# Merged-stage weights of a hybrid decoder layer: every second unit is split into high and low parts by two transfers from DRAM instead of by a load, ScalarE and VectorE

## The chip, the core and the metric

The kernel runs on one core of a Trainium2 chip. The metric is the time of one execution on the device in microseconds (us), the median of its runs. Engines are named as in the profile: PE (TensorE matmuls), PEld (its weight loads), DVE (VectorE), ACT (ScalarE), POOL (GpSimd) and SP (SyncE); POOL, SP and ACT also issue DMA transfers, each from a queue of its own.

## The reference

One layer on 256 tokens of width 2048, all in float32. The input projection feeds multi-head latent attention (16 heads) and a short gated convolution. Each branch has an output projection, both are merged by sigmoid gates, and one projection and a norm follow:

```python
h = _rmsnorm(x, pre_norm_g)
proj = jnp.einsum('bsd,de->bse', h, w_in)
(q_a, c_kv, k_rope, z_mla, c_in, b_gate, c_gate, z_conv, g_mla, g_conv) = jnp.split(proj, cuts, axis=-1)
...
y_mla = jnp.einsum('bse,ed->bsd', attn, w_o_mla)
...
y_conv = jnp.einsum('bse,ed->bsd', b_gate * conv * jax.nn.silu(z_conv), w_o_conv)
merged = jax.nn.sigmoid(g_mla) * y_mla + jax.nn.sigmoid(g_conv) * y_conv
out = jnp.einsum('bsd,de->bse', merged, w_out)
x = x + _rmsnorm(out, post_norm_g)
```

The four 2048 x 2048 weights of `g_mla`, `g_conv`, `y_mla` and `y_conv` are those of the merged stage.

## The kernel before

**Products by parts.** TensorE takes float32r operands, which hold fewer bits than float32. So each operand is split into a high part (the value rounded to float32r) and a low part (value minus high part), and a product is three matmuls: high by high, high by low, low by high (`product`). The low part of a weight tile is `wlo`, the high part `whi`.

**Units.** All weights are cut into 193 units of 128 partitions x 2048 columns (1 MB), numbered in the order of use (`plan`, some are smaller). `load_raw` issues the load of a unit into a `raw` tile (three buffers) from SP's queue. `split_unit` makes two halves of 1024 columns: for each, ACT writes `whi` by a copy that rounds (`split_act`, line 245 in the profile), and DVE writes `wlo` by a subtraction (line 246). `whi` and `wlo` have five buffers each, one per half, used in turn. `take(i)` asks for the raw loads up to unit i+2 and the splits up to unit i+1, then hands the pieces to the matmuls; all matmuls are issued at line 88.

**Stages.** Units 0 to 12 serve the latent projections, 13 to 112 the heads and the convolution, 113 to 176 the merged stage, 177 to 192 the output projection. The merged stage goes over four columns c of 512 outputs; a column has 16 units, four for each of n = 0 (g_mla), 1 (g_conv), 2 (w_o_mla) and 3 (w_o_conv). `tokens(c, n, cols)` takes the four units kk of one n. A unit holds four blocks of 128 x 512; for t = 0 and t = 1 (128 tokens each) the four blocks are gone through, three matmuls each: 24 matmuls a unit, that read half 0, half 1, half 0, half 1. At the end of a column DVE merges the two token blocks into `sg` tiles and turns them (line 320), and POOL writes each to DRAM in four transfers (`far<-sg`, line 328) and reads it back (`sg<-far`, line 332), all within `turned`.

**Order.** A scheduler sets the order on each engine and adds the semaphore waits; every instruction made under `keep_in_program_order` keeps its place on its engine, as all matmuls and all of POOL's transfers here do. Each engine then goes through its list in that order: an instruction that waits holds those behind it. A tile is given out again when all that read it have finished.

Of the kernel before, what the change touches and what calls it, by code (L numbers as in the profile page):

```python
# [11 lines left out]
F32 = mybir.dt.float32  # L12
F32R = mybir.dt.float32r
I32 = mybir.dt.int32
AF = mybir.ActivationFunctionType
ALU = mybir.AluOpType
PSUM = bass.MemoryType.PSUM

P = 128
# [18 lines left out]
UNIT = 2048  # L38
LINE = 32
HALF = UNIT // 2  # L40
# [42 lines left out]
def tile_layer(ctx: ExitStack, tc: tile.TileContext, xw, w0, xb, x, pos, pvec, post_g, wc, wz, wcv, wkr, wqk, wqr, wv, cwr, wsq, out):  # L83
    nc = tc.nc
# [13 lines left out]
    wpool = ctx.enter_context(tc.tile_pool(name="wpool", bufs=1))  # L98
# [5 lines left out]
    plan = []  # L104

    def add(ap, width=UNIT):
        plan.append((ap, width))
        return len(plan) - 1
# [30 lines left out]
    u_d = [[[add(wsq[n, c, k]) for k in range(4)] for n in range(4)] for c in range(4)]  # L139
# [3 lines left out]
    u_out = {ck: add(wsq[4, ck[0], ck[1]]) for ck in out_order}  # L143

    raws, splits, early = {}, {}, {}
    done = {"raw": 0, "split": 0}

    def load_raw(i):
        ap, w = plan[i]
        t = early.get(i)  # L150
        if t is None:
            t = wpool.tile([P, UNIT], F32, name=f"raw{i}", tag="raw", bufs=3)
        if i == 0:
            pieces = [(S, XW, w0), (XW, 2 * XW, xb[0])]
        elif i in (1, 2):

            pieces = [(j * XW, (j + 1) * XW, xb[2 * i - 1 + j]) for j in range(2)]
        else:
            pieces = [(0, w, ap)]
        for a, b, piece in pieces:  # L160
            nc.sync.dma_start(out=t[:, a:b], in_=piece)
        raws[i] = t
        if i == u_qa[5]:
            tc.keep_in_program_order(nc.sync.dma_start(out=tables_pi, in_=pos))
        if i == u_ckv[1]:
            tc.keep_in_program_order(nc.sync.dma_start(out=x_tok, in_=x))

    def split_unit(i):
        t, w = raws.pop(i), plan[i][1]
        parts = []  # L170
        if i == u_kr:
            t = t[:, :w].rearrange("p (k c) -> p k c", k=KD)
            for h in range(2):
                both = wpool.tile([P, HALF], F32R, name=f"whi{i}_{h}", tag="whi", bufs=5)
                both = both[:, :].rearrange("p (k j c) -> p k j c", k=KD // 2, j=2)
                ks = slice(h * KD // 2, (h + 1) * KD // 2)
                split_act(both[:, :, 0], both[:, :, 1], t[:, ks])
                parts.append(both.rearrange("p k j c -> p k (j c)"))
            splits[i] = parts
            return  # L180
        if i <= u_qa[-1]:

            hi, lo = (wpool.tile([P, HALF], F32R, name=f"{o}{i}", tag=o, bufs=5) for o in ("whi", "wlo"))
            for j in range(2):
                k, o = 2 * i + j, j * XW
                src = x_first if k == 0 else t[:, o : o + S]
                split_scaled(x_both, src, k)
                split_act(hi[:, j * R : (j + 1) * R], lo[:, j * R : (j + 1) * R], t[:, o + S : o + XW], True)
            splits[i] = [(hi, lo)]
            return  # L190
        for h in range(0, w, HALF):
            n = min(HALF, w - h)
            if u_out[3, 0] <= i < u_out[3, 3]:
                hi, lo = (op.tile([P, HALF], F32R, name=f"w{o}{i}_{h}") for o in ("hi", "lo"))
            else:
                hi = wpool.tile([P, HALF], F32R, name=f"whi{i}_{h}", tag="whi", bufs=5)
                lo = wpool.tile([P, HALF], F32R, name=f"wlo{i}_{h}", tag="wlo", bufs=5)
            split_act(hi[:, :n], lo[:, :n], t[:, h : h + n], i == u_head[0][1], i in (u_grp["r", 0], u_grp["v", 0], u_head[0][0]))
            parts.append((hi, lo))
        splits[i] = parts  # L200

    def ahead(i, raw=3, split=1):
        while done["raw"] < min(i + raw, len(plan)):
            load_raw(done["raw"])
            done["raw"] += 1
        while done["split"] < min(i + 1 + split, len(plan)):
            while done["raw"] <= done["split"]:
                load_raw(done["raw"])
                done["raw"] += 1
            split_unit(done["split"])  # L210
            done["split"] += 1
# [32 lines left out]
    def split_act(hi, lo, src, keep=False, later=False):  # L244
        a = nc.scalar.activation(hi, src, AF.Copy)  # L245
        b = nc.vector.tensor_tensor(lo, src, hi.bitcast(F32), op=ALU.subtract)  # L246
        if keep:

            tc.keep_in_program_order(a)
        if keep or later:  # L250
            tc.keep_in_program_order(b)
# [91 lines left out]
    def split_scaled(dst, src, k):  # L343
        if k < 3:

            a = nc.vector.tensor_scalar(dst[:, k, :S], src, col("pre_g", k), None, op0=ALU.mult)
        else:
            a = nc.scalar.activation(dst[:, k, :S], src, AF.Copy, scale=col("pre_g", k))
        tc.keep_in_program_order(a)
        tc.keep_in_program_order(  # L350
            nc.vector.scalar_tensor_tensor(
                dst[:, k, S:], src, col("pre_g", k), dst[:, k, :S].bitcast(F32), op0=ALU.mult, op1=ALU.subtract
            )
        )
# [839 lines left out]
```

## Time and profile before

| | |
|---|---|
| median of 2 runs | 1034.59 us (1034.59 to 1034.6) |
| profiled execution, first to last instruction | 1032.9 us |
| busy in it: PE, PEld | 1026.4 us, 854.6 us |
| busy in it: DVE, ACT, POOL | 687.9 us, 531.3 us, 174.2 us |
| mean granted TensorE clock | 0.999 |
| read from HBM, written | 215.66 MB, 12.58 MB |
| packets of SP's queue, of POOL's queue | 54.4%, 8.9% of the 16 DMA engines' time |

The median lies 1.7 us above the span of the profiled execution: that much of a run lies outside its first and last instruction. Busy time is the union of an engine's instructions, and a matmul's end is modelled, so that PE's share says that work never stopped rather than how fast it went. In lists of groups, `out<-in` names tiles without buffer numbers; the numbers behind the bar are busy time in us, mean ns of one instruction, then the idle time ahead of them and what ended it. In lists of transfers the last number is the median time from issue to landing in us.

### The profile page before, as it was taken

To read this page: it belongs to the slowest core of one execution; us is meant where nothing else is said; L and a number is where in the kernel's file an instruction comes from. 1 tells how busy PE (TensorE), PEld (TensorE's weight loads), DVE (VectorE), ACT (ScalarE), POOL (GpSimd) and SP (SyncE) were. 2 spreads that over 40 slices of the span, in tenths; PEclk is the share of its full clock that TensorE was granted. 3 is DMA by queue.
4 is the path that set the end of the run, shared out by engine and by line. 5 is a ranking of instruction groups with operands and counts; after the bars stand their busy time and mean duration, and the time that the engine had idled before them with its cause. 6 is when DMAs were issued, how large, how long until landed. Compare 5 with 4: busy or idle time off the path is not lost.

```text
span 1032.9 us, 12670 instructions
## 1 busy us (share of the span) xinstructions
PE 1026.4 (99%) x4648; PEld 854.6 (83%) x4648; DVE 687.9 (67%) x973; ACT 531.3 (51%) x750; POOL 174.2 (17%) x324
## 2 busy tenths in 40 slices
PE   9999999999999999999999999999999999999997
PEld 8888888888888888888888888888888888888886
DVE  7588777787687777777777785564455455455562
ACT  7675555655456464564555465344434444443551
POOL 4620421104210223112133120020010001002000
PEclk9999999999999999999999999999999999999999
DMA  9775766558675676857676765565565556558642
GB/s 356 280 257 214 269 215 227 207 191 297 212 252 193 209 279 210 278 184 242 229 271 222 267 217 200 204 222 188 201 218 208 188 202 243 183 187 335 231 165 81
DMA packets 44669, 233.24 MB, mean 226 GB/s; under 512 B 7968, under 2 KB 10656, under 8 KB 21696
## 3 DMA queue, kind: packets, MB, share of 16 engines
q1 hardware_dynamic: 32544, 199.67, 54.4%
q0 software_dynamic: 11632, 29.48, 8.9%
q10 hardware_dynamic: 432, 3.29, 0.8%
q8 instruction: 36, 0.59, 0.2%
q14 instruction: 25, 0.20, 0.1%
HBM read 215.66 MB, written 12.58 MB: 221 GB/s over the span
## 4 chain that ended last, share of the span: by engine, by line
PE 99%; DVE 0%; ACT 0%; issue 0%
PE cv L88 34%; PE sq L88 34%; PE z L88 8%; PE out L88 8%; PE qa L88 2%; PE kn L88 2%; PE qn L88 2%; PE vv L88 2%; PE ckv L88 2%; PE qr L88 1%; PE o L88 1%; PE sw L88 1%; PE sc L88 1%; PE idle L88 0%; PE kr L88 0%; DVE og L1048 0%
## 5 line engine op out<-in xcount | busy, mean ns | idle before, releaser
L246 DVE TENSOR_TENSOR wlo<-raw,whi 128x1024 fp32r<-128x1024 f32 (+1 forms) x370 | 440.5, 1196 | 276.6 <-ACT whi L245 265.5
L245 ACT ACTIVATE whi<-raw 128x1024 fp32r<-128x1024 f32 (+1 forms) x372 | 382.7, 1035 | 412.2 <-PE sq L88 180.5
L88 PE MATMUL cv<-whi,x_both 128*128 128x512 f32 x1024 | 319.8, 389 | 0.0
L88 PEld LDWEIGHTS cv<-whi,x_both 128*128 128x128 f32 x1024 | 192.3, 188 | 39.6
L88 PE MATMUL cv<-wlo,x_both 128*128 128x512 f32 x512 | 199.4, 390 | 0.0
L88 PE MATMUL sq<-whi,x_both 128*128 128x512 f32 x512 | 158.2, 389 | 0.0
L88 PEld LDWEIGHTS sq<-whi,x_both 128*128 128x128 f32 x512 | 96.1, 188 | 19.8
L88 PEld LDWEIGHTS cv<-wlo,x_both 128*128 128x128 f32 x512 | 96.1, 188 | 19.3
L88 PE MATMUL sq<-wlo,x_both 128*128 128x512 f32 x256 | 99.6, 389 | 0.0
L88 PE MATMUL z<-whi,x_both 128*128 128x512 f32 x256 | 80.0, 389 | 0.0
L88 PE MATMUL sq<-whi,at_both 128*128 128x512 f32 x256 | 79.4, 389 | 0.0
L88 PE MATMUL sq<-whi,cv_both 128*128 128x512 f32 x256 | 79.4, 389 | 0.0
L88 PE MATMUL out<-whi,m_both 128*128 128x512 f32 x256 | 79.0, 389 | 0.0
L328 POOL DMA_DIRECT2D far<-sg x32 | 17.5, 553 | 305.8 <-DVE sg L320 232.6
L328 POOL DMA_DIRECT2D far<-via x64 | 35.2, 557 | 191.4 <-DVE via L320 190.0
L88 PEld LDWEIGHTS sq<-wlo,x_both 128*128 128x128 f32 x256 | 48.1, 188 | 10.0
L88 PEld LDWEIGHTS out<-whi,m_both 128*128 128x128 f32 x256 | 48.1, 188 | 10.0
L88 PEld LDWEIGHTS sq<-whi,cv_both 128*128 128x128 f32 x256 | 48.1, 188 | 9.9
L88 PEld LDWEIGHTS sq<-whi,at_both 128*128 128x128 f32 x256 | 48.1, 188 | 9.9
L88 PEld LDWEIGHTS z<-whi,x_both 128*128 128x128 f32 x256 | 48.1, 188 | 9.9
L88 PE MATMUL z<-wlo,x_both 128*128 128x512 f32 x128 | 49.8, 389 | 0.0
L88 PE MATMUL sq<-wlo,at_both 128*128 128x512 f32 x128 | 49.8, 389 | 0.0
(227 smaller groups left out, 1131.3 us busy)
## 6 DMA issues: line engine op xcount, KB each, us to landing
raw<-wsq_dram SPq DMA_DIRECT2D x80, 1024.0 KB, 4.8
raw<-wcv_dram SPq DMA_DIRECT2D x64, 1024.0 KB, 5.5
raw<-wz_dram SPq DMA_DIRECT2D x16, 1024.0 KB, 4.8
raw<-wqk_dram SPq DMA_DIRECT2D x8, 1024.0 KB, 6.1
cw<-cwr_dram POOLq DMA_DIRECT2D x24, 256.0 KB, 5.8
raw<-wc_dram SPq DMA_DIRECT2D x4, 1024.0 KB, 9.8
raw<-wv_dram SPq DMA_DIRECT2D x4, 1024.0 KB, 5.3
far<-via POOLq DMA_DIRECT2D x64, 48.0 KB, 4.1
```

The costliest lines, as they stand in the source:

```text
L88: return tc.keep_in_program_order(nc.tensor.matmul(*a, **kw))
L245: a = nc.scalar.activation(hi, src, AF.Copy)
L246: b = nc.vector.tensor_tensor(lo, src, hi.bitcast(F32), op=ALU.subtract)
L328: tc.keep_in_program_order(queue.dma_start(out=f[i], in_=m))
```

## The change

In the merged stage every unit with an odd number (32 of the 64: kk = 0 and 2 of each n) gets no raw load and no split by ACT and DVE. For each of its halves POOL issues a transfer from the weights in DRAM into the `whi` tile, whose type float32r is to round; ACT writes minus `whi` into `wlo`; then POOL issues a second transfer of the same weights that adds them to what stands in `wlo`. The even units are loaded and split as before, and the matmuls are the same.

```diff
     def load_raw(i):
         ap, w = plan[i]
+        if by_transfers(i):
+            return
         t = early.get(i)
...
+    def by_transfers(i):
+
+        return u_d[0][0][0] <= i < u_out[0, 0] and i % 2 == 1
+
+    def split_by_transfers(i):
+
+        ap, parts = plan[i][0], []
+        for h in range(0, UNIT, HALF):
+            hi = wpool.tile([P, HALF], F32R, name=f"whi{i}_{h}", tag="whi", bufs=5)
+            lo = wpool.tile([P, HALF], F32R, name=f"wlo{i}_{h}", tag="wlo", bufs=5)
+            src = ap[:, h : h + HALF]
+            tc.keep_in_program_order(nc.gpsimd.dma_start(out=hi[:, :], in_=src))
+            nc.scalar.activation(lo[:, :], hi[:, :].bitcast(F32), AF.Copy, scale=-1.0)
+            tc.keep_in_program_order(nc.gpsimd.dma_start(out=lo[:, :], in_=src, accum_op=ALU.add))
+            parts.append((hi, lo))
+        splits[i] = parts
+
     def split_unit(i):
+        if by_transfers(i):
+            split_by_transfers(i)
+            return
         t, w = raws.pop(i), plan[i][1]
```

The lines behind these move down by 22, so that ACT's copy of an even unit is line 267 after the change, DVE's subtraction 268, and POOL's turns 350 and 354; the new transfers are lines 181 and 183, the negation 182. In the names below `whi135_1024` is the high part of half 1 (columns 1024 on) of unit 135, and `far_6185` a tile in DRAM. DMASW are the semaphores of POOL's transfers, DMAHW those of SP's.

POOL's list at the end of column 0, from the second token block's turn on; before:

```order
L328 DMA far_6185<-sg1_1_5885 32x4x128 [waits DVE_49]
L328 DMA far_6185<-sg1_1_5885 32x4x128
L328 DMA far_6185<-sg1_1_5885 32x4x128 [waits DMASW1_49]
L328 DMA far_6185<-sg1_1_5885 32x4x128 [waits DMASW2_49]
L332 DMA sg0_0_5733<-far_6181 128x512 [waits DMASW5_49,DMASW6_49,DMASW4_49,DMASW3_49]
L332 DMA sg0_1_5735<-far_6185 128x512 [waits DMASW2_49,DMASW7_49,DMASW1_49,DMASW0_49]
L328 DMA far_6765<-sg1_0_6480 32x4x128 [waits DVE_49]
```

The same place after the change:

```order
L350 DMA far_6185<-sg1_1_5885 32x4x128 [waits DMASW6_49]
L354 DMA sg0_0_5733<-far_6181 128x512 [waits DMASW2_49,DMASW7_49,DMASW1_49,DMASW0_49]
L354 DMA sg0_1_5735<-far_6185 128x512 [waits DMASW5_49,DMASW6_49,DMASW4_49,DMASW3_49]
L181 DMA whi131_0_6232<-wsq_dram 128x1024 [waits PE_49]
L183 DMA wlo131_0_6233<-wsq_dram 128x1024 [waits Activation_49]
L181 DMA whi131_1024_6237<-wsq_dram 128x1024 [waits PE_49]
L183 DMA wlo131_1024_6238<-wsq_dram 128x1024 [waits Activation_49]
L181 DMA whi133_0_6300<-wsq_dram 128x1024 [waits PE_49]
```

Before, nothing followed a column's turn until the next column's. Now the transfers of units 131 to 145 stand between them, in pairs, the second of each behind a wait for ACT, and those of unit 131 behind the turn's waits.

ACT's list in column 1, units 135 to 137 (their place in the column is kk = 2, 3 and 0); before:

```order
L245 ACTIVATE whi135_0_6380<-raw135_6344 128x1024 [waits DMAHW7_49]
L245 ACTIVATE whi135_1024_6384<-raw135_6344 128x1024 [waits PE_49]
L245 ACTIVATE whi136_0_6414<-raw136_6378 128x1024 [waits DMAHW0_49,PE_49]
L245 ACTIVATE whi136_1024_6418<-raw136_6378 128x1024 [waits DVE_49,PE_49]
L245 ACTIVATE whi137_0_6448<-raw137_6412 128x1024 [waits DMAHW1_49,DVE_49,PE_49]
```

The same place after the change:

```order
L182 ACTIVATE wlo135_0_6379<-whi135_0_6378 128x1024 [waits DMASW1_49]
L267 ACTIVATE whi136_0_6412<-raw136_6376 128x1024 [waits DMAHW4_49,PE_49]
L182 ACTIVATE wlo135_1024_6384<-whi135_1024_6383 128x1024 [waits DMASW6_49,DMASW3_49]
L267 ACTIVATE whi136_1024_6416<-raw136_6376 128x1024 [waits PE_49]
L182 ACTIVATE wlo137_0_6447<-whi137_0_6446 128x1024 [waits DMASW5_49,DVE_49,PE_49]
```

The roundings of the even unit stand between the negations of the odd ones, and each negation waits for the landing of its first transfer.

POOL's list at the start of the stage; before:

```order
L777 DMA cw_5445<-cwr_dram 128x512 [waits DMASW6_49,DVE_49]
L328 DMA far_5551<-cw_5549 32x4x128 [waits DVE_49]
L328 DMA far_5551<-cw_5549 32x4x128 [waits DMASW2_49]
L328 DMA far_5551<-cw_5549 32x4x128 [waits DMASW3_49]
L328 DMA far_5551<-cw_5549 32x4x128 [waits DMASW4_49]
```

The same place after the change:

```order
L799 DMA cw_5445<-cwr_dram 128x512 [waits DMASW6_49,DVE_49]
L181 DMA whi113_0_5494<-wsq_dram 128x1024 [waits PE_49,Activation_49]
L183 DMA wlo113_0_5495<-wsq_dram 128x1024 [waits DMASW2_49,Activation_49]
L181 DMA whi113_1024_5499<-wsq_dram 128x1024 [waits DMASW3_49,PE_49]
L181 DMA whi115_0_5619<-wsq_dram 128x1024 [waits DMASW4_49,PE_49]
L183 DMA wlo113_1024_5500<-wsq_dram 128x1024 [waits DMASW5_49,Activation_49]
L183 DMA wlo115_0_5620<-wsq_dram 128x1024 [waits Activation_49]
L350 DMA far_5551<-cw_5549 32x4x128 [waits DMASW7_49,DVE_49]
```

The first transfers of units 113 and 115 stand behind the load of `cw`, and the turn of the last convolution block stands behind them.

## Prediction

> **What bounds the kernel now.** I read the page first: span, busy time, granted clock, and the chain that ended last.
>
> ```profile
> span 1032.9 us, 12670 instructions
> PE 1026.4 (99%) x4648; PEld 854.6 (83%) x4648; DVE 687.9 (67%) x973; ACT 531.3 (51%) x750; POOL 174.2 (17%) x324
> ...
> PEclk9999999999999999999999999999999999999999
> ...
> PE 99%; DVE 0%; ACT 0%; issue 0%
> ```
>
> TensorE works without a gap at its full clock, and the whole chain is TensorE. Nothing that relieves another engine can shorten it; the change can only leave the time alone or open gaps. So the question is whether the weights still arrive in time in the merged stage. Its stretch in the windows view, and the first matmul of column 0 and of column 1 in the timeline of PE:
>
> ```profile
> core 0: us, PE busy (x) PEld busy (x) DVE busy (x) ACT busy (x) POOL busy (x), PEclk, DMA share, GB/s
> 590.00:938.20 348.20, 348.20 (x1537) 288.38 (x1536) 192.78 (x190) 156.25 (x169) 22.29 (x41) 1.00 0.58 206
> ```
>
> ```profile
> 589.79 0.39 PE L88 MATMUL sq<-whi,x_both 128*128 128x512 f32 x1
> ...
> 676.87 0.39 PE L88 MATMUL sq<-whi,x_both 128*128 128x512 f32 x1
> ```
>
> Sixteen units take 676.87 − 589.79 = 87.08 us, so one unit is U = 5.44 us. A unit is read in quarters, half 0, half 1, half 0, half 1 (t = 0, then t = 1). Half 0's buffers come free at 3/4 of the unit, half 1's at its end. The waits of the stage and ACT's timeline show that the splits do wait for these releases, not for weights:
>
> ```profile
> ACT whi L245 <- PE sq L88: 180.2, 109, 3.0
> DVE wlo L246 <- ACT whi L245: 146.7, 70, 2.9
> ```
>
> ```profile
> 675.71 1.06 ACT L245 ACTIVATE whi<-raw 128x1024 fp32r<-128x1024 f32 x1 [3.02 <-PE sq L88]
> 677.07 1.06 ACT L245 ACTIVATE whi<-raw 128x1024 fp32r<-128x1024 f32 x1 [0.30 <-PE sq L88]
> 681.15 1.06 ACT L245 ACTIVATE whi<-raw 128x1024 fp32r<-128x1024 f32 x1 [3.02 <-PE sq L88]
> ```
>
> 677.07 − 675.71 = 1.36 us is a quarter unit, 681.15 − 675.71 = 5.44 a unit. With five buffers, half 0 of unit i takes the buffer of half 1 of unit i−3, free two units (10.88 us) ahead of need. Half 1 takes that of half 0 of unit i−2: free at 3/4 of i−2, needed at 1/4 of i, a lead of one and a half units, 8.16 us. Today a split is 1.06 + 1.22 us of that lead, because the raw weights already lie in SBUF.
>
> **The change, part by part.** It removes 64 subtractions on DVE and 32 loads on SP; from the groups of the stage:
>
> ```profile
> L245 ACT ACTIVATE whi<-raw 128x1024 fp32r<-128x1024 f32 x129 | 136.7, 1059 | 181.0 <-PE sq L88 177.6 <-PE out L88 3.3
> ...
> L246 DVE TENSOR_TENSOR wlo<-raw,whi 128x1024 fp32r<-128x1024 f32 x130 | 159.1, 1224 | 153.0 <-ACT whi L245 147.8
> ```
>
> 64 × 1.224 = 78 us of DVE, all beside TensorE: worth 0. ACT trades 64 roundings for 64 negations of the same shape, priced alike at 1.06 us: 0 by itself. POOL gains 128 transfers, some 0.57 us each to issue (73 us, beside a POOL that is busy for 22 of 348 us). What costs is the order. A half is now made by a chain that starts only when its buffer is free: first transfer (l1, issue to landing), negation, second transfer (l2). I add 0.1 us for each of the two handovers, an estimate, so the negation counts 1.26 us. The five buffers, enough for 2.3 us of splitting, now have to cover two DMA latencies.
>
> l1 and l2 have no row: no 512 KB transfer stands on POOL's queue, and none rounds or adds. The nearest ones, from the list of issues (KB each, median us to landing), then two single ones from narrow windows:
>
> ```profile
> q1 hardware_dynamic: 32544, 199.67, 54.4%
> ...
> raw<-wsq_dram SPq DMA_DIRECT2D x80, 1024.0 KB, 4.8
> ...
> sg<-far POOLq DMA_DIRECT2D x8, 256.0 KB, 5.3
> ...
> at_f<-far_qa SPq DMA_DIRECT2D x1, 512.0 KB, 5.3
> ```
>
> ```profile
> sg<-far POOLq DMA_DIRECT2D x1, 256.0 KB, 3.1
> ```
>
> ```profile
> sg<-far POOLq DMA_DIRECT2D x1, 256.0 KB, 6.9
> ```
>
> SP's queue moves 199.67 MB in 0.544 × 1032.9 us, 355 GB/s, so another 256 KB is 0.74 us. By the sg rows a plain 512 KB transfer then takes 3.8 to 7.6 us, 6.0 at the median. I take l1 = 5.3: the sg rows were measured with a raw load in flight for 4.8 of every 5.44 us, and with half the raw loads I give the 0.74 us back. The second transfer must also read what it adds to: another 512 KB, 1.5 us at the same rate, so l2 = 6.8. Ends: 3.8 for both (reading the target costs nothing) and 7.6 and 9.1; above that no row sets an end if rounding or adding is slow in itself. A gain is excluded, since TensorE has no gap to lose.
>
> Steady state. From the release of half 0 of unit i−2 to half 1 of unit i being ready: l1 + 1.26 + l2; TensorE meets it at 1/4 of unit i, and gives the next buffer of this loop free at 3/4, U/2 = 2.72 us later. So two units take at least 3.98 + l1 + l2 = 16.1 us instead of 10.88: a gap of 5.2 us in every second unit. POOL's queue alone (first transfer, wait for the negation, second issue, twice) needs 2 × (5.3 + 1.26 + 0.57) = 14.3 us, less than that. The DMA engines have, at 355 GB/s, 2.95 us of raw load, 5.9 of the four transfers and 2.95 of targets read in that time, 11.8 us: less as well, though over today's 10.88. 32 × 5.2 = 166 us.
>
> The rounding of the even units stands behind negations that wait for a landing, but its halves have a lead of 8.16 us and more, and need 2.3: cost 0 while the period is stretched anyway.
>
> Column ends. POOL issues unit 129, then both turns of sg, then unit 131 (145 and 147, 161 and 163 alike). The turns in POOL's timeline:
>
> ```profile
> 677.11 2.20 POOL L328 DMA_DIRECT2D far<-sg  x4 [70.77 <-ACT whi L245]
> 681.40 2.17 POOL L328 DMA_DIRECT2D far<-sg  x4 [2.09 <-DVE sg L320]
> 684.21 0.57 POOL L332 DMA_DIRECT2D sg<-far  x1 [0.64 <-DMA far<-sg]
> 688.38 0.57 POOL L332 DMA_DIRECT2D sg<-far  x1 [3.60 <-DMA far<-sg]
> ```
>
> POOL waits for DVE and for landings (the last for 3.60 us) and is free at 688.95, 12.1 us after the column's end at 676.87. Only then starts unit 131: its half 1 is ready 12.1 + 2 × 5.3 + 6.8 + 3.1 (two negations of 1.26 and one issue of 0.57) = 32.6 us after the column's end. With steady gaps alone TensorE would be there after 2.25 U + 2 × 5.2 = 22.6: 10.0 us more, three times, 30 us. The turn after the last column has no transfer behind it.
>
> Start of the stage. Unit 113 stands behind a load of cw on POOL:
>
> ```profile
> 583.22 0.55 POOL L777 DMA_DIRECT2D cw<-cwr_dram  x1 [8.77 <-DVE mv L793]
> ```
>
> From 583.8, half 1 is ready at 583.8 + 10.6 + 6.8 + 3.1 = 604.3, needed at 591.2: 13.1 us, 7.9 over the steady gap.
>
> Sum: 166 + 30 + 8 = 204 us. The profiled span of 1032.9 becomes 1237; the median of the timed runs lies 1.7 above that span, so 1239, said as **1240**.
>
> **The rivals.**
> *Fast transfers.* Every transfer lands like the fastest sg row, 3.8 us for 512 KB. Then two units take 3.98 + 7.7 = 11.7, a gap of 0.8: 25 us; column ends 12.1 + 11.5 + 3.1 − 12.2 − 1.6 = 12.9 each, 39; start 6: about 1105. For it: half the raw loads are gone. Against it: each second transfer shares the engines with the first transfer that POOL issues 0.57 us behind it, and the median of the eight sg rows, at half the bytes, is 5.3.
> The Trainium skill's page "DMA: Bandwidth & Descriptors", section "Anatomy of one DMA — SWDGE (gpsimd) path", gives about 2.0 us plus bytes/436e3 for a transfer from GpSimd: an estimate of 3.2 us for 512 KB, which would leave no steady gap and only the column ends and the start, about 1078 in all. For 256 KB it gives 2.6, and the trace's rows are 3.1 to 6.9; the trace does not bear it out here, and this goes into the same rival.
>
> *Slow rounding or adding.* The nearest rows are plain copies. At 7.6 and 9.1 us two units take 20.7: gaps 9.8, 314 us, column ends 8 each, start 10: 1382. If rounding and adding cost a further 1.5 us each (9.1 and 10.6), two units take 23.7 and the same sum gives about 1475. The profile holds no transfer that rounds or adds, so nothing in it speaks against this; for it speaks only that these are the one kind of work here that no row prices.
>
> *Not slower.* If POOL hands a transfer over with its wait and goes on, no transfer stands behind another's wait, column ends and start cost nothing, and only the loop of half 1 is left. It decides when l1 + 1.26 + l2 is under 8.16 us, so l1 + l2 under 6.9: then 1035. Against it: POOL's 3.60 us idle ahead of sg<-far is such a wait, held on the engine, and even the fastest row doubled is 7.7.
>
> That the first transfer copies bits and rounds nothing would leave wlo at zero and every transfer and wait in place: the same time.
>
> **How the numbers follow.** My case (1150 to 1330 by itself) has 0.55; fast transfers 0.15; slow rounding or adding 0.27; not slower 0.03. The range 1080 to 1430 leaves out the not-slower case and the upper half of the slow one, 0.17 together. A measurement of this kernel can tell about 2% from no change; that is 21 us, and only the last rival stays under it: slower 0.97, same 0.02, faster 0.01.
>
> **What would show it.** The profile after should have PE waits on second transfers (DMA wlo<-wsq_dram) totalling near 200 us, nearly all between 590 and the stage's end, in 32 places at half 1 of odd units; two units 16 us apart; first transfers landing in 5.3 us, second ones in 6.8; three longer gaps of some 15 us behind the sg turns; a TensorE clock as before, DVE 78 us less busy, ACT unchanged. A wrong l1 or l2 moves the time by 32 us per microsecond and more. The prediction is wrong in kind if TensorE waits for even units (ACT's order), or if POOL's queue sets the period of two units.

## The result, and the profile after

| | before | after |
|---|---|---|
| median of 2 runs | 1034.59 us | 1329.14 us (1327.26 to 1331.02) |
| ratio to before, 95% interval | | 1.2848 [1.2804, 1.2891] |
| profiled execution, first to last instruction | 1032.9 us | 1325.5 us |
| merged stage, by its matmuls | 348.2 us | 641.6 us |
| PE busy in it, PE idle in it | 348.2 us, 0 | 424.7 us, 216.9 us |

The page of the kernel after: span, busy time, the slices of PE and of its granted clock, then the chain that ended last.

```profile
span 1325.5 us, 12740 instructions
...
PE 1101.9 (83%) x4648; PEld 896.5 (68%) x4648; DVE 611.0 (46%) x909; ACT 528.7 (40%) x750; POOL 264.9 (20%) x452
...
PE   9999999999999999985676668666475665776998
...
PEclk9999999999999999997888887888787887888999
...
PE 57%; issue 22%; DMA 12%; POOL 4%; ACT 2%; DVE 1%; POOLq 0%; ACTq 0%
```

The first 17 slices are as before; in those of the merged stage, PE works four to eight tenths of the time, and its clock is no longer full. In the chain, DMA, POOL, ACT and issues stand where PE alone stood. The merged stage in the windows view of the kernel after (columns as before):

```profile
core 0: us, PE busy (x) PEld busy (x) DVE busy (x) ACT busy (x) POOL busy (x), PEclk, DMA share, GB/s
589.20:1230.80 641.60, 424.69 (x1539) 331.33 (x1539) 121.53 (x131) 159.90 (x174) 112.57 (x168) 0.82 0.63 165
```

The stage is 641.6 − 348.2 = 293.4 us longer, the whole difference of the spans (292.6). Of this 641.6 − 424.7 = 216.9 us is idle PE, and 424.7 − 348.2 = 76.5 us is the same matmuls taking longer: the granted clock fell from 1.00 to 0.82. What was waited for in the stage, by the waits view (us in total, times, longest):

```profile
POOL wlo L183 <- ACT wlo L182: 434.9, 58, 10.0
...
ACT wlo L182 <- DMA whi<-wsq_dram: 341.0, 53, 16.9
...
PE sq L88 <- DMA wlo<-wsq_dram: 214.1, 38, 8.6
ACT whi L267 <- PE sq L88: 118.1, 44, 11.7
...
POOL whi L181 <- PE sq L88: 16.7, 16, 1.8
```

This is to be read from the bottom of the chain up. PE waits 214 us for second transfers, 38 times. POOL stands 435 us with the second transfer in hand, waiting for the negation; ACT stands 341 us for the first transfer to land. The last row is the telling one: POOL waits only 16.7 us for a buffer. The new transfers in the list of issues:

```profile
raw<-wsq_dram SPq DMA_DIRECT2D x48, 1024.0 KB, 7.0
whi<-wsq_dram POOLq DMA_DIRECT2D x64, 512.0 KB, 6.4
wlo<-wsq_dram POOLq DMA_DIRECT2D x64, 512.0 KB, 5.5
```

One cycle of two units in POOL's timeline (start, duration, idle time ahead and what ended it), and PE and ACT in it:

```profile
1027.02 0.56 POOL L181 DMA_DIRECT2D whi<-wsq_dram  x1 [1.03 <-PE sq L88]
1034.53 0.87 POOL L183 DMA_DIRECT2D wlo<-wsq_dram  x1 [6.96 <-DVE wlo L268]
1035.09 0.85 POOL L181 DMA_DIRECT2D whi<-wsq_dram  x1
1045.43 0.86 POOL L183 DMA_DIRECT2D wlo<-wsq_dram  x1 [9.48 <-ACT wlo L182]
1047.36 0.56 POOL L181 DMA_DIRECT2D whi<-wsq_dram  x1 [1.08 <-PE sq L88]
```

```profile
1042.71 0.80 PE L88 MATMUL sq<-wlo,cv_both 128*128 128x512 f32 x1 [7.59 <-DMA wlo<-wsq_dram]
```

```profile
1032.22 1.06 ACT L267 ACTIVATE whi<-raw 128x1024 fp32r<-128x1024 f32 x1 [2.97 <-PE sq L88]
1033.19 1.04 ACT L182 ACTIVATE wlo<-whi 128x1024 fp32r<-128x1024 f32 x1
1044.07 1.06 ACT L182 ACTIVATE wlo<-whi 128x1024 fp32r<-128x1024 f32 x1 [9.84 <-DMA whi<-wsq_dram]
```

Apart from the 1.08 us at its end, in which POOL waits for a buffer, it issues one transfer or holds the other back all through this cycle of 20.3 us. The cycle is one of column 2; in the other columns two units take about 18.4 us. (The second row names DVE; ACT's negation ended at 1034.23, 0.30 us before the issue.) PE stands for 7.59 us of it.

### The profile page after: what moved, and what is told of

Read it like the earlier page. It is cut to its first block, busy times and chain, and to the rows that moved or that the text cites. A ratio compares the mean times of both kernels' runs of the same rounds, so it can differ in the third digit from the quotient of the medians.

```text
span 1325.5 us, 12740 instructions
## 1 busy us (share of the span) xinstructions
PE 1101.9 (83%) x4648; PEld 896.5 (68%) x4648; DVE 611.0 (46%) x909; ACT 528.7 (40%) x750; POOL 264.9 (20%) x452
## 4 chain that ended last, share of the span: by engine, by line
PE 57%; issue 22%; DMA 12%; POOL 4%; ACT 2%; DVE 1%; POOLq 0%; ACTq 0%
PE cv L88 26%; PE sq L88 7%; PE z L88 7%; PE out L88 7%; DMA wlo<-wsq_dram 6%; DMA whi<-wsq_dram 5%; POOL wlo L183 2%; PE kn L88 2%; PE qa L88 2%; PE qn L88 2%; POOL whi L181 2%; PE vv L88 2%; PE ckv L88 2%; PE qr L88 1%; ACT wlo L182 1%
## 5 line engine op out<-in xcount | busy, mean ns | idle before, releaser
L268 DVE TENSOR_TENSOR wlo<-raw,whi 128x1024 fp32r<-128x1024 f32 (+1 forms) x306 | 361.4, 1191 | 510.0 <-ACT whi L267 505.0
L267 ACT ACTIVATE whi<-raw 128x1024 fp32r<-128x1024 f32 (+1 forms) x308 | 314.2, 1029 | 346.1 <-PE cv L88 125.4
L88 PE MATMUL sq<-wlo,x_both 128*128 128x512 f32 x256 | 117.5, 459 | 117.9 <-DMA wlo<-wsq_dram 117.9
L182 ACT ACTIVATE wlo<-whi 128x1024 fp32r<-128x1024 f32 x64 | 67.6, 1057 | 359.2 <-DMA whi<-wsq_dram 341.0
L88 PE MATMUL sq<-whi,x_both 128*128 128x512 f32 x512 | 182.6, 440 | 2.1 <-DMA whi<-wsq_dram 2.1
L183 POOL DMA_DIRECT2D wlo<-wsq_dram x64 | 55.7, 870 | 479.0 <-ACT wlo L182 434.9
L88 PEld LDWEIGHTS sq<-wlo,x_both 128*128 128x128 f32 x256 | 56.5, 221 | 139.5 <-DMA wlo<-wsq_dram 127.5
L88 PEld LDWEIGHTS sq<-whi,x_both 128*128 128x128 f32 x512 | 113.2, 221 | 28.7 <-DMA whi<-wsq_dram 3.6
L88 PE MATMUL sq<-wlo,cv_both 128*128 128x512 f32 x128 | 57.8, 451 | 48.6 <-DMA wlo<-wsq_dram 48.6
L88 PEld LDWEIGHTS sq<-wlo,cv_both 128*128 128x128 f32 x128 | 27.9, 218 | 58.4 <-DMA wlo<-wsq_dram 52.2
L88 PEld LDWEIGHTS sq<-wlo,at_both 128*128 128x128 f32 x128 | 27.4, 214 | 57.2 <-DMA wlo<-wsq_dram 51.1
```

The costliest lines, as they stand in the source:

```text
L88: return tc.keep_in_program_order(nc.tensor.matmul(*a, **kw))
L182: nc.scalar.activation(lo[:, :], hi[:, :].bitcast(F32), AF.Copy, scale=-1.0)
L183: tc.keep_in_program_order(nc.gpsimd.dma_start(out=lo[:, :], in_=src, accum_op=ALU.add))
```

## Experiments

In the table, the stage and PE's busy time in it are those of the windows view, idle is their difference, and the transfers are the medians of the lists of issues. Before, the stage is 348.2 us and PE busy throughout.

| kernel | us | ratio to before | stage | PE busy | PE idle | first, second transfer |
|---|---|---|---|---|---|---|
| after | 1329.1 | 1.2848 [1.2804, 1.2891] | 641.6 | 424.7 | 216.9 | 6.4, 5.5 |
| e1, one unit in four | 1210.9 | 1.1703 [1.1660, 1.1746] | 521.1 | 392.5 | 128.6 | 5.9, 5.5 |
| e2, both first transfers together | 1234.8 | 1.1933 [1.1909, 1.1957] | 548.8 | 409.3 | 139.5 | 6.1, 6.9 |
| e3, six buffers | 1319.6 | 1.2753 [1.2726, 1.2781] | 606.1 | 429.2 | 176.9 | 6.5, 5.5 |
| e4, e2 and e3 | 1238.1 | 1.1948 [1.1894, 1.2001] | 515.0 | 396.7 | 118.3 | 8.1, 5.7 |
| e5, 20 matmuls in each gap | 1328.0 | 1.2859 [1.2815, 1.2903] | 641.8 | 542.2 | 99.6 | 6.6, 5.5 |
| e12, 30 matmuls in each gap | 1321.5 | 1.2776 [1.2747, 1.2804] | 632.8 | 585.3 | 47.5 | 6.8, 5.5 |
| e10, turns on SP | 1325.2 | 1.2802 [1.2781, 1.2823] | 638.9 | 421.4 | 217.5 | 6.9, 5.6 |
| e8, second transfer adds nothing | 1248.2 | 1.2067 [1.2043, 1.2091] | 562.5 | 412.4 | 150.1 | 5.1, 4.3 |
| e7, second transfer only | 1126.6 | 1.0891 [1.0810, 1.0973] | 447.5 | 383.2 | 64.3 | –, 7.6 |
| e6, first transfer only, VectorE subtracts | 1094.0 | 1.0576 [1.0537, 1.0615] | 404.5 | 366.7 | 37.8 | 6.1, – |
| e11, no second transfer | 1078.4 | 1.0422 [1.0399, 1.0446] | 389.5 | 358.6 | 30.9 | 5.4, – |
| e9, raw loads from POOL | 1056.1 | 1.0206 [1.0181, 1.0231] | 367.5 | 355.6 | 11.9 | 4.9 (plain) |

The edits are shown against the kernel after, but for e9's, which is to the kernel before. In e6 and e7 `load_raw` is that of the kernel before as well, and `split_by_transfers` takes the unit's raw tile (`t = raws.pop(i)`).

**Two transfers in a row, or one?** e6 keeps the raw load of odd units and lets VectorE subtract; e7 keeps it too, and ScalarE rounds and negates from it, so that only the adding transfer is left. e6's edit:

```diff
-            tc.keep_in_program_order(nc.gpsimd.dma_start(out=hi[:, :], in_=src))
-            nc.scalar.activation(lo[:, :], hi[:, :].bitcast(F32), AF.Copy, scale=-1.0)
-            tc.keep_in_program_order(nc.gpsimd.dma_start(out=lo[:, :], in_=src, accum_op=ALU.add))
+            tc.keep_in_program_order(nc.gpsimd.dma_start(out=hi[:, :], in_=ap[:, h : h + HALF]))
+            nc.vector.tensor_tensor(lo[:, :], t[:, h : h + HALF], hi[:, :].bitcast(F32), op=ALU.subtract)
```

> Odd units keep their raw load; whi comes by the first (rounding) transfer, wlo by VectorE's subtraction of whi from raw, and there is neither a negation nor a second transfer. Theory: one transfer of 4 to 5 us and 1.3 us of VectorE fit in the lead of 8.16 us, so no steady gap; unit 131 and its like still stand behind the sg turns (12.1 + 5 + 1.3 = 18.4 us after a column's end, needed after 10.9) : three gaps of 7 to 8 us: about 1060 (1045 to 1085). Rival (rounding in a transfer is slow by itself, over 7 us): steady gaps, 1100 or more.

and e7's:

```diff
-            tc.keep_in_program_order(nc.gpsimd.dma_start(out=hi[:, :], in_=src))
+            nc.scalar.activation(hi[:, :], t[:, h : h + HALF], AF.Copy)
             nc.scalar.activation(lo[:, :], hi[:, :].bitcast(F32), AF.Copy, scale=-1.0)
-            tc.keep_in_program_order(nc.gpsimd.dma_start(out=lo[:, :], in_=src, accum_op=ALU.add))
+            tc.keep_in_program_order(nc.gpsimd.dma_start(out=lo[:, :], in_=ap[:, h : h + HALF], accum_op=ALU.add))
```

> Odd units keep their raw load and ScalarE's rounding; ScalarE also writes the negation, and only the second (adding) transfer follows. Theory: 1.06 + 1.06 + 5.5 = 7.8 us with handovers, just inside the lead of 8.16: no steady gaps or very small ones, three gaps behind the sg turns: about 1060 (1040 to 1090). Rival (adding is what costs): steady gaps, 1100 or more.

Measured 1094.0 and 1126.6 us, both above what was expected, and e7 lies where its rival was put (adding is what costs: steady gaps, 1100 or more). PE's waits in e7:

```profile
PE sq L88 <- DMA wlo<-wsq_dram: 64.3, 36, 5.4
```

So the adding transfer alone does open steady gaps, but short ones: 64.3 us in 36 waits, against 214.1 in 38 in the kernel after. With one transfer in the chain the stage loses 404.5 − 348.2 = 56 and 99 us, with two in a row 293, nearly twice the sum: the serial order of the two is the larger part of the cost, as forecast. In e7 the raw load of every unit is in flight beside the adding transfer, whose median is 7.6 us there against 5.5.

**Is rounding or adding slow in itself?** e8 leaves `accum_op` out, e11 the whole second transfer, and e9 puts two plain 512 KB transfers on POOL's queue in place of the raw load of odd units, in the kernel before.

```diff
-            tc.keep_in_program_order(nc.gpsimd.dma_start(out=lo[:, :], in_=src, accum_op=ALU.add))
+            tc.keep_in_program_order(nc.gpsimd.dma_start(out=lo[:, :], in_=src))
```

> The second transfer writes the rounded weights instead of adding the weights to the negation; the addition is left out. Everything else, order and waits, is the same. If adding costs about a further read of the target, the second transfer lands in some 4.3 instead of 5.5 us, and the first one behind it sooner by as much: 32 x (1.2 to 2.4) less, about 1270 (1240 to 1300). If adding costs nothing, 1329.

```diff
-            tc.keep_in_program_order(nc.gpsimd.dma_start(out=lo[:, :], in_=src, accum_op=ALU.add))
```

> The changed kernel without the second transfer: wlo stays the negation, so the low part of the odd units is wrong by the weights themselves (the addition is left out). POOL's chain has no negation in it any more, and a half needs 4.0 to 5 + 1.3 us against a lead of 8.16: no steady gaps, some at the three column ends (12.1 + 5 + 1.3 against 10.9): about 1060 (1040 to 1080). The landing of its first transfers, beside those of e9, prices the rounding; that of the changed kernel less this one prices the place behind the second transfer (6.4 us there).

```diff
+        if u_d[0][0][0] <= i < u_out[0, 0] and i % 2 == 1:
+            for h in range(0, UNIT, HALF):
+                tc.keep_in_program_order(nc.gpsimd.dma_start(out=t[:, h : h + HALF], in_=ap[:, h : h + HALF]))
+            raws[i] = t
+            return
```

> The kernel before, with the raw weights of the odd merged-stage units loaded by two plain transfers of 512 KB from POOL's queue instead of one of 1 MB from SP's; the splits are unchanged. Three raw buffers give a lead of more than two units, so the time should stay near before: 1035 to 1050, with some more behind the sg turns. It prices a plain transfer on this queue, beside e11 with the same bytes in the stage: if rounding costs nothing, the landings are alike (4.0 to 4.5 us undisturbed); if rounding is slow, plain ones land over 1 us sooner.

The rows in the lists of issues, of e8, of e11 and of e9 (KB each, median us to landing):

```profile
whi<-wsq_dram POOLq DMA_DIRECT2D x64, 512.0 KB, 5.1
wlo<-wsq_dram POOLq DMA_DIRECT2D x64, 512.0 KB, 4.3
```

```profile
whi<-wsq_dram POOLq DMA_DIRECT2D x64, 512.0 KB, 5.4
```

```profile
raw<-wsq_dram POOLq DMA_DIRECT2D x64, 512.0 KB, 4.9
```

Without the addition the second transfer lands in 4.3 instead of 5.5 us, and the first one that follows it on the queue in 5.1 instead of 6.4: adding costs some 1.2 us twice. The time falls by 81 us of the 295, to where it was expected. Nothing shows rounding to be slow: the fastest transfer that rounds lands in 3.7 us, the fastest plain one in 4.1. The medians, 5.4 and 4.9, come from kernels with other transfers beside them and price nothing by themselves. e11's 1078.4 us lies in its expected range; 27.0 of its 30.9 us of idle PE are three gaps behind the turns of sg. e9 shows in addition what is left when nothing stands in a chain: 21 us over before, 11.9 of it idle PE, most of it behind the turns of sg at the ends of columns 0 to 2, where POOL is held as forecast. e9 missed its expectation by a few us; there the matmuls' clock is 0.98, and PE is busy for 7 us more.

**Half as many such units.**

```diff
-        return u_d[0][0][0] <= i < u_out[0, 0] and i % 2 == 1
+        return u_d[0][0][0] <= i < u_out[0, 0] and i % 4 == 1
```

> Sixteen units (kk = 0 of each n) instead of 32 take the two transfers. Theory (latency): each such unit starts its chain when its buffer comes free and must pass two transfers within the lead of five buffers, so a gap of about 6.8 us (4.1 + 1.3 + 0.6 + 6.2 + 1.3 + 5.5 = 19.0 us from the release, needed after 12.2) and about 2 us of half clock behind it remain at each: 16 x 8.9 = 142, about 1175 us (1130 to 1200). Rival (throughput: POOL's queue or the DMA engines cannot carry four more transfers per two units): the queue needs some 16.5 us per odd unit and now has 21.8, so the gaps vanish: 1035 to 1060.

Measured 1210.9 us, above the expectation. Each such unit costs (521.1 − 348.2) / 16 = 10.8 us, more than the 293.4 / 32 = 9.2 of the kernel after, although there are half as many. So it is a latency that is paid per unit, and not a rate of bytes. Here it is the buffers that hold POOL, as its waits show:

```profile
POOL whi L181 <- PE sq L88: 198.2, 14, 17.4
```

With four units between two such units the loop of the buffers binds; in the kernel after the same row has 16.7 us.

**Buffers, or POOL's queue?** Two circles run through the same transfers: the five buffers (release of half 0, the chain of half 1, the matmuls to the next release) and POOL's queue (first transfer, negation, second issue, for each half in turn). e2 issues both first transfers of a unit ahead of both second ones; e3 has six buffers of `whi` and `wlo`, paid for with two raw buffers instead of three; e4 has both.

```diff
-            src = ap[:, h : h + HALF]
-            tc.keep_in_program_order(nc.gpsimd.dma_start(out=hi[:, :], in_=src))
-            nc.scalar.activation(lo[:, :], hi[:, :].bitcast(F32), AF.Copy, scale=-1.0)
-            tc.keep_in_program_order(nc.gpsimd.dma_start(out=lo[:, :], in_=src, accum_op=ALU.add))
+            tc.keep_in_program_order(nc.gpsimd.dma_start(out=hi[:, :], in_=ap[:, h : h + HALF]))
...
+        for h, (hi, lo) in zip(range(0, UNIT, HALF), parts):
+            nc.scalar.activation(lo[:, :], hi[:, :].bitcast(F32), AF.Copy, scale=-1.0)
+            tc.keep_in_program_order(nc.gpsimd.dma_start(out=lo[:, :], in_=ap[:, h : h + HALF], accum_op=ALU.add))
```

> POOL issues the first transfers of both halves, then the two second ones; nothing else changes. If POOL's queue (first transfer, wait for the negation, second, twice) sets the period, its cycle falls to about 10 us and the gaps all but vanish: 1035 to 1080. If the loop of half 1 (buffer free at 3/4 of unit i-2, two transfers and a negation, needed at 1/4 of unit i) sets it, the chain is still 11 to 13 us against a lead of 8.16: gaps of 3 to 5 us plus the slow clock, about 1215 (1170 to 1260).

```diff
-            t = wpool.tile([P, UNIT], F32, name=f"raw{i}", tag="raw", bufs=3)
+            t = wpool.tile([P, UNIT], F32, name=f"raw{i}", tag="raw", bufs=2)
...
-            hi = wpool.tile([P, HALF], F32R, name=f"whi{i}_{h}", tag="whi", bufs=5)
-            lo = wpool.tile([P, HALF], F32R, name=f"wlo{i}_{h}", tag="wlo", bufs=5)
+            hi = wpool.tile([P, HALF], F32R, name=f"whi{i}_{h}", tag="whi", bufs=6)
+            lo = wpool.tile([P, HALF], F32R, name=f"wlo{i}_{h}", tag="wlo", bufs=6)
```

> Six whi and wlo buffers instead of five, two raw buffers instead of three to make room; the order stays. Leads become 12.24 us for both halves. If the loop of half 1 alone sets the gaps, they fall from about 7 to 3 us: about 1180. If POOL's queue is as tight (2 x (6.4 + 1.3 + 0.6) = 16.6 us per two units), they fall only to some 5.5: about 1270 (1230 to 1290). A bound by DMA bandwidth leaves 1329. The two raw buffers may cost a few us at the start of the kernel.

> Six buffers and both first transfers ahead of the second ones. Theory (latency against lead, in the queue and in the buffers): half 1 is ready 14 to 15 us after its release, needed after 13.6: gaps of about 1 us, too short for the clock to fall; with column ends and start about 1090 (1060 to 1130). Rival (the transfers' throughput): no gain over the better one of the two edits alone, and the slow clock stays.

The merged stage in the windows view, of e3 and of e4:

```profile
619.20:1225.30 606.10, 429.21 (x1537) 334.80 (x1537) 122.11 (x132) 160.96 (x173) 110.72 (x166) 0.82 0.66 175
```

```profile
624.70:1139.70 515.00, 396.66 (x1537) 309.22 (x1537) 121.13 (x129) 156.17 (x172) 112.61 (x166) 0.89 0.77 205
```

Both stages begin 30 to 36 us late (619.2 and 624.7 against 589.2): the other numbers of buffers cost that before the merged stage, so the times of e3 and e4 mislead, and the stages are to be compared. From 641.6, e3 takes 35 us, e2 93 and e4 127, about the sum of the two. With six buffers POOL waits for no buffer any more (its waits name PE's matmuls nowhere), and the stage still takes 606 us: that is POOL's queue alone. Changing only the order on that queue (e2) brings nearly three times as much as e3, whose 35 us are not the sixth buffer's alone, since its two raw buffers also change when raw loads run.

e2's time lies where the buffers' loop was expected to set it (1170 to 1260), and so it does once the queue's circle is shorter. POOL's waits in e2:

```profile
POOL whi L181 <- PE sq L88: 238.9, 29, 13.1
```

The two circles are thus near each other: the queue alone holds the stage at 606 us, and the buffers still hold it at 549 when the queue's is shortened. e3 and e4 missed their expectations, e4 by over 100 us. By its time, which is no better than e2's, e4 is what its rival said (the transfers' throughput); only the stages, 515.0 against 548.8 us, show a gain. First transfers land after 8.1 us there, and the DMA engines are busy for 0.77 of the stage against 0.63 in the kernel after. How far their load limits e4 was not tried.

**The turns of sg taken off POOL.**

```diff
-            steps.append(turned(m[t][:, :], y[:, :], 4))
+            steps.append(turned(m[t][:, :], y[:, :], 4, None, nc.sync))
```

> The changed kernel with the sg turns at the column ends issued from SP's queue instead of POOL's. Theory (POOL's queue is one serial chain that sets the stage's time: 64 x (6.73 landing + 1.64 to the second issue + 1.78 to the next first issue) = 650 us against 641 measured): the three turns hold that queue for 10.5, 11.2 and 12.2 us between the units, 32 us over an ordinary step, and all of it comes back: about 1297 (1288 to 1310). Rival (the buffers' loop through PE sets it): the turns come back only as far as the gaps of units 131, 147 and 163 exceed their neighbours', about 16 us: 1313; none at all: 1329.

Measured 1325.2 us, its interval overlapping that of the kernel after: no gain that can be told. So the simple theory, that POOL's queue is a fixed sum from which the turns can be taken, fell. POOL's timeline, summed over the 63 halves whose two issues stand apart, shows where the time went: from first issue to second, 527.8 us in the kernel after and 550.0 in e10; from second issue to the next first, 100.5 and 76.7. The turns are gone from the second sum, but POOL then meets buffers that are not free, and the first sum grew by about as much. The wait for buffers in e10 (16.7 us in 16 waits in the kernel after):

```profile
POOL whi L181 <- PE sq L88: 24.2, 19, 2.3
```

**Is it the clock?** Matmuls on data that is there already fill each gap, into a bank that nothing reads; they keep PE busy, so that its clock does not fall.

```diff
+FILL = 20
...
+                    if by_transfers(u_d[c][n][kk]) and t == 0 and k4 == 2:
+                        fill = bank(f"fill{c}_{n}_{kk}", tag="st", bufs=1)
+                        for _ in range(FILL):
+                            matmul(fill[:, :], x_both[:, 0, :P], x_both[:, 0, :], start=True, stop=True)
```

> Twenty matmuls of 512 columns whose result nobody reads (x_both by itself, into a free bank) stand in PE's list ahead of the second quarter of each of the 32 odd units, where PE waits for wlo: 32 x 20 x 0.227 = 145 us more work. Theory: the TensorE clock halves because of the gap of 4 to 9 us, so with 4.5 us of it filled the granted clock stays near 1 and the 67 us lost to slow matmuls come back, while the gaps' end is set by the transfers as before: about 1255 (1235 to 1285). Rival (the clock falls for another reason, or the added work adds to the time): 1329 or more.

The same with `FILL = 30`:

> As e5, with 30 added matmuls (6.8 us) at each odd unit, 218 us more work for PE. Theory (POOL's chain sets the time, TensorE and its clock are beside it): the time stays at 1329 (1322 to 1345), the granted clock goes to 0.97 or more. Rival (the slow clock is part of the time): it falls below 1300. Rival (TensorE's work is part of the time): it rises to 1400 or more.

The merged stage in the windows view, of e5 and of e12:

```profile
589.60:1231.40 641.80, 542.23 (x2177) 431.07 (x2177) 121.76 (x131) 158.75 (x173) 112.28 (x168) 0.93 0.64 165
```

```profile
589.50:1222.30 632.80, 585.26 (x2498) 472.76 (x2497) 121.89 (x131) 156.77 (x173) 111.47 (x167) 0.97 0.65 167
```

With 960 matmuls more, PE is busy for 585 of 633 us at a clock of 0.97, and the kernel takes 1321.5 us, 8 less than without them. So the slow clock is not what the time is made of: the 76 us by which the matmuls grew lie beside transfers that PE would otherwise have waited for. e5's expectation, in which the clock was part of the time, fell. Its time is that of its rival, in which the added work adds to the time, but e12, with half as much again, is no slower. e12 came out just below its expected range.

Why does PE's being ready sooner bring so little? By POOL's timelines, a first transfer issued within 1 us of a second one is followed by its own second after 8.86 us on average (41 of them in the kernel after), one issued later after 7.54 (21). Two things are mixed in this. Beside 20 of the 41, but only 3 of the 21, a raw load of an even unit is in flight for 3.5 us or more, and these 23 land after 8.4 us on average. With no raw load beside them (0.5 us at most), the 14 right behind an adding transfer land after 6.2 us and the 18 later ones after 5.1; in e8, where the second transfer adds nothing, the same two groups land after 5.1 (7 of them) and 4.7 (19). So an adding transfer ahead holds the next one up by about 1 us, and a raw load beside it by some 2 more.

In e12 POOL waits for a buffer only once, for 0.6 us, and 56 first transfers stand right behind a second one. Summed over the 63 halves, the step from second issue to the next first is 20.0 us shorter than in the kernel after, and the step from first to second 15.4 us longer. What PE gives back in waits of up to 1.8 us, the queue takes again for the most part.

## Why the prediction was right in direction and short in size

**Right.** The kernel is slower, and in the main for the reason named: a half made by two transfers, one behind the other, comes too late for TensorE. PE waits for second transfers (214.1 us in 38 waits, forecast near 200), by the distances of matmul starts nearly all at half 1 of odd units (202.5 us in 32 places). DVE is 76.9 us less busy (forecast 78), ACT 2.6 us; even units cost no idle PE. The time, 1329, lies in the range, but 89 us above the 1240, at the very end of the 1150 to 1330 that its own case was given.

**What failed.** The step that failed is "POOL's queue alone … 14.3 us, less than that": the queue was put below the 16.1 us of the loop of half 1 and left out of the sum. So the lead of five buffers is not what mainly binds. The prediction named a period set by POOL's queue as the sign of being wrong in kind, and in this it was: POOL waits for buffers for 16.7 us only, e3 without such waits still takes 606 of 641 us, and 527.8 / 63 = 8.38 us per half instead of 5.3 + 1.26 = 6.56 make it 2 × (8.38 + 0.56) = 17.9 us for two units, and 19.9 on average with the turns, the start and the waits for buffers. What the terms measured:

| term | forecast | measured | why |
|---|---|---|---|
| l1, first transfer | 5.3 | 6.4 median, 6.7 mean | two in three follow an adding transfer within 1 us on the same queue, which costs about 1 us; a raw load in flight beside 23 of the 64 makes it 8.4; 5.1 in e8, which adds nothing |
| negation and handovers | 1.26 | 1.64 mean, 1.44 median, landing to second issue | the two handovers take more than 0.2; in ACT's rows above the negation also stands behind the even unit's rounding (1032.22, then 1033.19) |
| l2, second transfer | 6.8 | 5.5 median, 5.9 mean | adding costs 1.2 us (e8), where 1.5 was put for reading the target; the transfer without it lands in 4.3, not 5.3 |
| issue ahead of the next first transfer | 0.57 | 0.56, but 0.87 long | the adding transfer takes 0.87 us on POOL, the next one starts beneath it |
| matmuls from quarter to 3/4 of a unit | 2.72 | 4.4 mean, up to 4.9 | the clock is half after a gap (from half 1's first matmul with `wlo` to the fourth quarter) |

By the measured terms the loop of half 1 at full clock is 2.72 + 6.7 + 1.64 + 5.5 = 16.6 us, near the forecast 16.1: errors of opposite sign cancelled there. With the 4.4 us that the matmuls took at their slow clock it is 18.2, level with the queue's 17.9. In POOL's queue l2 does not appear, only l1 and the negation, both set too low, so nothing cancelled. e8 fits this: from first to second issue its sum over 63 halves is 448.4 us, 79.4 less than 527.8, and its stage is 79.1 us shorter. But the steps on the queue add up to the stage whatever sets them, so this says where the time went; that the queue holds the stage nearly as long without the buffers rests on e3 and e12, in which POOL hardly waits for one.

The idle time came out near its forecast, 216.9 us for 204, by luck: two units took 3.8 us longer than forecast (19.9 for 16.1), and 76.5 / 32 = 2.4 us of that was filled by slow matmuls, which no term had.

**The clock.** "A TensorE clock as before" was wrong. Windows of the kernel after, around the cycle above:

```profile
1043.00:1047.00 4.00, 4.00 (x12) 3.15 (x13) 0.00 (x0) 1.06 (x1) 0.86 (x1) 0.61 0.10 26
1047.00:1053.00 6.00, 6.00 (x28) 4.96 (x27) 1.23 (x1) 1.49 (x2) 0.56 (x1) 1.00 0.77 174
```

Behind the 7.59 us gap 12 matmuls take 4.0 us (0.33 us each); then 28 take 6.0 (0.21). The Trainium skill's page "TensorE: Matmul & The Clock Gate", section "HAM oscillation — how this bites in real kernels", tells of it: gaps of more than some 3.4 us while waiting for a DMA put TensorE back to half its clock, and it starts cold each time. The trace agrees: the granted clock has a step of 0.5 at nearly every gap, most of them 3.4 to 10.2 us long. Shorter gaps have such steps too, those of 2.5 and 2.7 us in the kernel after and 16 of 1.8 to 3.2 us in e5, so 3.4 us is no lower end here. But the section counts half of the throttled time as lost, and here e12 gave back 8 us of 76: where a queue elsewhere sets the pace, slow matmuls only take the place of waiting.

**Column ends and start.** Forecast 30 and 8 us. POOL was held as forecast: 10.5 to 12.2 us between a second issue and the next first at the three turns. But idle PE at the starts of units is 22.5 us in all the stage, the gaps of units 131, 147 and 163 were 8.2, 15.4 and 9.0 us where some 15 each was forecast, and taking the turns off POOL gave nothing measurable (e10). The place was right, the price was not additive.

**What stays open.** In e10 both kinds of first transfers became slower (9.19 and 7.89 us to the second issue, against 8.86 and 7.54), with the turns on SP's queue; why was not tried apart. Column 2 takes 20.4 us per two units between its ends and the others 18.4. The trace shows what differs: in column 2 the raw load of an even unit is issued together with the second transfer of half 1 (1034.6 and 1034.53 us in the cycle above), which then lands after about 8.1 us instead of 5.5. What sets them going together was not tried. How the 293 us divide between queue and buffers, beyond e2, e3 and e4, is not settled. A first transfer on another queue than POOL's wasn't tried.

None of these kernels reaches the kernel before, whose PE had no gap to fill.

## What to carry to other kernels

Where a transfer's issue waits for the landing of another on the same in-order queue, price the queue's whole circle, landing and handover and issue for each piece, beside the circle of the buffers, and give each its own latencies: a transfer right behind another on its queue, or beside a load on another queue, lands later than a lone one. When two such circles are near each other in length, relieving the shorter one, or the clock of the engine that waits, returns little; look for the one that has no idle time of its own.

## What the runs showed of the hardware

- A 512 KB transfer from DRAM into SBUF that adds to its target lands in 5.5 us against 4.3 for the same transfer without the addition, and holds POOL for 0.87 against 0.54 us at its issue.
- A 512 KB transfer that rounds float32 to float32r shows no cost of its own beside a plain one: fastest 3.7 and 4.1 us, issue 0.540 and 0.537 us; the medians, 5.4 and 4.9, have other transfers beside them.
- An adding transfer also holds up the next one on its queue: with no raw load in flight, a 512 KB transfer lands after 6.2 us right behind one and after 5.1 later, against 5.1 and 4.7 where the transfer ahead adds nothing. A raw load of 1 MB from SP's queue, in flight beside it for 3.5 us or more, makes it 8.4.
- Most of PE's waits of 2.5 to 8.6 us bring its granted clock to 0.5, mostly for 3.4 to 10.2 us; filler matmuls keep it at 0.97 but bring 8 us of 295.
